# One stock of places for raw weights and their split parts, and a last phase in another order

## The chip, the cores and the metric

The kernel runs on one core of a Trainium2 chip. The core has five engines that run their own instruction streams and wait for one another through semaphores: TensorE (PE in the profile) multiplies matrices, VectorE (DVE) and ScalarE (ACT) work elementwise, GpSimd (POOL) does the same and issues indirect DMAs, SyncE (SP) issues the loads of weights. The metric is the time of one launch on the device in microseconds (us). Three runs of the kernel before took 1482.25, 1484.7 and 1488.44 us; the median is 1484.7.

## The reference

One decoder layer for 512 tokens of width 1024 in float32:

```python
hn = rmsnorm(h, g_mix_norm);  u = hn @ w_in + b_in
ret = silu(rg) * rmsnorm(retention(rq, rk, rv), ret_norm_g)      # 4 heads of 128, chunks of 128
att = sliding_window_attention(aq, ak, av, sinks, bias_table)    # 8 heads of 64, window 128
h = h + concatenate([ret, att]) @ w_out
h = h + moe(rmsnorm(h, g_moe_norm), ...)                         # top 4 of 32 experts
gate = sigmoid(h @ w_ple_gate)
h = h + rmsnorm(gate * (p @ w_ple_proj), g_ple_norm)
return rmsnorm(h, g_final)

def expert(xblk, e):                      # in moe, for the rows routed to expert e
    h = xblk @ w_up[e] + b_up[e]          # 1024 -> 2048
    return clamped_swiglu(h) @ w_down[e] + b_down[e]             # 1024 -> 1024
```

An expert has 8 MB of up weights and 4 MB of down weights, so the 32 experts read 384 MB.

## The kernel before, in words

**Stages.** Input projection, retention and attention take the first 280 us. Then come the output projection w_out, the router and the routing, then the loop over 32 experts, and last the projection of p, the gates and the two closing norms.

**Pieces.** All weights come in pieces of 1 MB (128 partitions x 2048 floats) in one fixed list, `pieces`: per expert eight up pieces and four down pieces, in the list as up(e+1), down(e). `prefetch` takes a raw place from the list `free` and issues the next load on SP's queue; `next_piece` and `whole_piece` take the oldest loaded piece and put its place back behind its last use. There are 3 + 5 + 4 raw places, from the pools rawp, raw2 and raw3.

**Two kinds of experts.** Experts are sorted by their number of tokens when the kernel runs. The table `BIG` says, place by place, which are L (up to 96 rows) and which S (up to 64 rows). An S expert's matmuls read the raw float32 piece directly, in pairs of 64 columns (`pairs64`). For an L expert each piece is split first (`split`): ACT copies it to float32r as wh, DVE subtracts it from the raw piece and writes the remainder wl. PE then makes three products: xTh x wh, xTl x wh and xTh x wl (in a down piece aTh and aTl take the place of xTh and xTl, and a piece holds two blocks of 128 rows, which are done one after the other). The parts wh and wl have pools of their own, whp and wlp with three buffers each, which are used in turn.

**Order.** The program is written out expert by expert: up(e), activation, transposes of the inputs of expert e+1 (`prep` or `prep64`), down(e-1), scatter of its rows into acc, transposes of the activation (`act_t` or `act_t64`). A scheduler orders each engine's instructions from that, with `issue_after` as hints. Each engine runs its own list strictly in that order.

**The end.** At e == E the kernel loads p, splits it, and issues the loads of w_ple_proj and two gate pieces only after the y of expert 30 (`prefetch(after=y)`). It makes three of four projections, reads a flag and branches around a general path for overfull experts, makes the fourth projection, and then runs the gates (i, c) for four token tiles i and two column halves c, with the closing norms (`finish`) between them.

Of the kernel before, what the change touches and what calls it, by code (L numbers as in the profile page):

```python
# [11 lines left out]
F32 = mybir.dt.float32  # L12
# [10 lines left out]
P = 128  # L23
# [13 lines left out]
RAW1, RAW2, RAW3 = 3, 5, 4  # L37
# [9 lines left out]
BIG = [c == "L" for c in "LL" + "SLSLSLSLSLSLSLL" + "SLSLSLSLSLSLLLS"]  # L47
# [48 lines left out]
def hymba_kernel(ctx, tc, x, p, positions, rel_bias_table, g_mix_norm, w_in, b_in, ret_norm_g,  # L96
# [27 lines left out]
    rawp = pool(ctx, "rawp", RAW1)  # L124
    whp = pool(ctx, "whp", 3)
    wlp = pool(ctx, "wlp", 3)
# [7 lines left out]
    R = SimpleNamespace(eid={})  # L134
    free = [rawp] * RAW1

    def raw_tile(dt=F32):
        pl_ = free.pop(0)
        return pl_.tile([P, 2048], dt, name="raw"), pl_

    def split(raw, parts=None, dst=None):
        if dst is None:
            wh = whp.tile([P, 2048], F32R, name="wh")
            wl = wlp.tile([P, 2048], F32R, name="wl")
        else:
            wh, wl = dst
# [51 lines left out]

    pieces = [w_ret(0, 0), w_ret(0, 4), w_kv, w_half(w_in, 0, 2048), w_half(w_in, 4, 2048)]
# [17 lines left out]
    def prefetch(after=None):  # L217
        if free and state["next"] < min(len(pieces), state["limit"]):
            t, pl_ = raw_tile()
# [3 lines left out]
            queue.append((t, pl_))  # L223
            state["next"] += 1

    def next_piece(parts=None, dst=None, more=True):
        t, pl_ = queue.pop(0)
        r = split(t, parts, dst)
        free.append(pl_)
# [3 lines left out]

    def whole_piece(use):

        t, pl_ = queue.pop(0)
        use(t)
        free.append(pl_)
# [88 lines left out]
    raw3 = pool(ctx, "raw3", RAW3)  # L327
    mix = [raw3.tile([P, 2048], F32R, name="raw").rearrange("p (a k t) -> a p k t", a=2, k=KD) for _ in range(NT)]
# [6 lines left out]
    p1 = px.enter_context(ExitStack())  # L335
    actp = pool(p1, "actp")
# [9 lines left out]
    prefetch()  # L346
    nc.sync.dma_start(out=xts[1], in_=x_v[:, 1, :])
    prefetch()
# [116 lines left out]
    def attention(nb):  # L465
# [8 lines left out]
        for gp in range(2):  # L474

            s_ps = [sps.tile([P, 512], F32, name="s_ps").rearrange("p (a b) -> p a b", a=2) for _ in range(2)]
            for g in range(2):
# [800 lines left out]
```

## Time and profile before

| | |
|---|---|
| median of 3 runs | 1484.7 us (1482.25 to 1488.44) |
| profiled execution | 1485.38 us |
| its span, first to last instruction | 1483.6 us |
| mean granted TensorE clock | 0.958 of full speed |
| DMA | 462.47 MB, mean 312 GB/s |

The page gives the busy time of each engine over the span, the costliest groups of instructions and the loads. A query of the trace gives stretches (`windows`: the busy time of each engine in a stretch, the granted clock and the share of the DMA engines) and single instructions (`timeline`: start, duration, and in square brackets how long the engine stood idle before and which instruction released it). A granted clock of 1.00 is 2.4 GHz, 0.50 is 1.2 GHz. Matmuls are pipelined: the time from one start to the next is what one costs, and its duration has the way through the array in it as well.

### The profile page before, as it was taken

What the parts mean: (1) busy time and instruction counts of PE and PEld (TensorE: products, weight loads), DVE (VectorE), ACT (ScalarE), POOL (GpSimd) and SP (SyncE); (2) the same over time, 40 slices, a digit from 0 to 9 for tenths busy, and PEclk for the clock granted to TensorE, in tenths of its full rate; (3) what the DMA queues carried; (4) which work ended last, traced back from release to release, by engine and by line L of the source; (5) the groups of instructions that cost most, each with busy time, mean ns of one, the idle gap of its engine ahead of it and who ended that gap; (6) DMA issues with size and microseconds to landing.
All of it is one profiled execution on the core that took longest, in us unless ns stands there. A gap on an engine that the chain in (4) does not pass through costs nothing. (4 is left out here: it accounts for less than half of the span.)

```text
span 1483.6 us, 16861 instructions
## 1 busy us (share of the span) xinstructions
PE 1351.3 (91%) x6090; PEld 907.1 (61%) x6091; DVE 830.1 (56%) x1005; ACT 677.7 (46%) x750; POOL 224.4 (15%) x238
## 2 busy tenths in 40 slices
PE   5999999588999999999999999999999999999885
PEld 4777777466657474655647657465655647675564
DVE  6637774776547263544637647354553726683356
ACT  5333443455536253543626535343452625573443
POOL 2213241474100000000000000000100000000023
PEclk9999999788999999999999999999999999999998
DMA  9332046667899999999999999999999999987511
GB/s 272 118 109 58 29 142 254 237 254 280 318 402 396 403 405 396 406 399 393 392 396 408 393 388 387 375 403 396 386 394 399 395 387 400 391 328 283 183 72 43
DMA packets 110427, 462.47 MB, mean 312 GB/s; under 512 B 10830, under 2 KB 29180, under 8 KB 77568
## 3 DMA queue, kind: packets, MB, share of 16 engines
q1 hardware_dynamic: 99584, 436.24, 74.8%
q0 software_dynamic: 10320, 24.52, 6.5%
q8 instruction: 49, 0.80, 0.2%
q10 hardware_dynamic: 432, 0.57, 0.1%
q14 instruction: 42, 0.34, 0.1%
HBM read 447.26 MB, written 18.73 MB: 314 GB/s over the span
## 5 line engine op out<-in xcount | busy, mean ns | idle before, releaser
L151 DVE TENSOR_TENSOR wl<-raw,wh 128x2048 fp32r<-128x2048 f32 (+2 forms) x243 | 530.2, 2222 | 151.8 <-ACT wh L150 143.8
L150 ACT ACTIVATE wh<-raw 128x2048 fp32r<-128x2048 f32 (+2 forms) x243 | 442.9, 1858 | 110.2 <-PE up L847 52.2
L864 PE MATMUL up<-raw,xTh 128*64 128x512 f32 x896 | 195.3, 594 | 0.0
L896 DVE TENSOR_SCALAR a<-up 128x512 f32<-128x512 f32 x50 | 32.9, 687 | 267.8 <-ACT sg L895 267.8
L847 PE MATMUL up<-wh,xTh 128*128 128x512 f32 x576 | 162.8, 405 | 9.2 <-ACT wh L150 7.8
L895 ACT ACTIVATE sg<-up 128x512 f32<-128x512 f32 x50 | 27.9, 595 | 297.0 <-issue 158.5
L847 PE MATMUL up<-wl,xTh 128*128 128x512 f32 x576 | 160.9, 401 | 2.2 <-DVE wl L151 2.2
L847 PE MATMUL up<-wh,xTl 128*128 128x512 f32 x576 | 161.0, 401 | 1.4 <-DVE xTl L292 1.4
L864 PEld LDWEIGHTS up<-raw,xTh 128*64 128x64 f32 x896 | 63.1, 137 | 124.6 <-issue 120.0
L847 PEld LDWEIGHTS up<-wh,xTh 128*128 128x128 f32 x576 | 108.7, 191 | 40.5 <-ACT wh L150 13.1
L847 PEld LDWEIGHTS up<-wl,xTh 128*128 128x128 f32 x576 | 109.0, 191 | 32.8 <-DVE wl L151 7.0
L847 PEld LDWEIGHTS up<-wh,xTl 128*128 128x128 f32 x576 | 109.8, 191 | 28.2 <-DVE xTl L292 1.8
L928 PE MATMUL dn<-wh,aTh 128*128 128x512 f32 x288 | 100.8, 434 | 23.8 <-ACT wh L150 23.8
L928 PE MATMUL dn<-wl,aTh 128*128 128x512 f32 x288 | 104.0, 446 | 15.9 <-DVE wl L151 15.9
L942 POOL DMA_INDIRECT acc<-y,slot_i x30 | 45.4, 1514 | 443.3 <-ACT y L937 434.8
L800 POOL DMA_INDIRECT xe<-xg,slot_i x30 | 31.9, 1064 | 485.9 <-PE dn L857 261.0
L864 PE MATMUL dn<-raw,aT 128*64 128x512 f32 x448 | 102.9, 598 | 0.0
L928 PE MATMUL dn<-wh,aTl 128*128 128x512 f32 x288 | 98.2, 425 | 0.0
L928 PEld LDWEIGHTS dn<-wh,aTh 128*128 128x128 f32 x288 | 59.4, 211 | 42.8 <-ACT wh L150 27.3
L928 PEld LDWEIGHTS dn<-wl,aTh 128*128 128x128 f32 x288 | 58.5, 212 | 35.5 <-DVE wl L151 23.1
L914 DVE SCALAR_TENSOR_TENSOR aTl<-tp,aTh 128x512 fp32r<-128x512 f32 x36 | 24.1, 689 | 90.2 <-ACT aTh L913 90.2
L928 PEld LDWEIGHTS dn<-wh,aTl 128*128 128x128 f32 x288 | 59.3, 206 | 15.0
(340 smaller groups left out, 1571.9 us busy)
## 6 DMA issues: line engine op xcount, KB each, us to landing
raw<-in_w_up_dram SPq DMA_DIRECT2D x256, 1024.0 KB, 17.4
raw<-in_w_down_dram SPq DMA_DIRECT2D x128, 1024.0 KB, 17.9
raw<-in_w_in_dram SPq DMA_DIRECT2D x32, 256.0 KB, 4.8
raw<-in_w_out_dram SPq DMA_DIRECT2D x4, 1024.0 KB, 5.0
raw<-in_w_ple_gate_dram SPq DMA_DIRECT2D x4, 1024.0 KB, 10.4
raw<-in_w_in_dram SPq DMA_DIRECT2D x3, 1024.0 KB, 5.7
xt<-in_x_dram SPq DMA_DIRECT2D x4, 512.0 KB, 6.5
h<-in_x_dram POOLq DMA_DIRECT2D x4, 512.0 KB, 7.6
```

The lines of the kernel that those rows point to most:

```text
L150: R.split_act = nc.scalar.activation(to(wh), src(raw), AF.Copy)
L151: R.split_dve = nc.vector.tensor_tensor(out=to(wl), in0=src(raw), in1=to(wh).bitcast(F32), op=ALU.subtract)
L800: return nc.gpsimd.indirect_dma_start(out=dst[0:n, 0:D // h], out_offset=None, in_=xg.rearrange("s (h d) -> (s h) d", h=h), in_offset=bass ...
L847: nc.tensor.matmul(h[n // 2][:, n % 2 * 512:n % 2 * 512 + 512], lhsT=a[:, k, :], rhs=w[:, n * 512:(n + 1) * 512], start=(k == 0 and a is x ...
L864: R.pair = nc.tensor.matmul(o[v * 64:v * 64 + 64, c:c + 512], lhsT=xT[:, k, :], rhs=w[:, v * n + c:v * n + c + 512], start=False, stop=las ...
L895: nc.scalar.activation(sg[:, cs], hv[:, :, 0], AF.Silu, scale=ALPHA)
L896: nc.vector.tensor_scalar(a[:, cs], hv[:, :, 1], LIMIT + 1.0, 1.0 - LIMIT, op0=ALU.min, op1=ALU.max)
L914: nc.vector.scalar_tensor_tensor(flat(l[:, g4, :]), in0=flat(t), scalar=1.0 / ALPHA, in1=flat(h[:, g4, :]).bitcast(F32), op0=ALU.mult, op1 ...
L928: m = nc.tensor.matmul(o[:, n * 512:(n + 1) * 512], lhsT=a[:, k, :], rhs=w[:, kk * 1024 + n * 512:kk * 1024 + (n + 1) * 512], start=False, ...
L942: nc.gpsimd.indirect_dma_start(out=acc.rearrange("s (h d) -> (s h) d", h=h), out_offset=bass.IndirectOffsetOnAxis(ap=idx[0:n, :], axis=0), ...
```

## The change

**One stock.** raw2 has nine places instead of five, and wlp is gone after the first phase. The raw places, the three places of whp and the four of mix (raw3) are 19 places in one stock with two lists, `free` and `spare`. A load takes from `free` first and then from `spare`. A split takes a place each for wh and wl, from `spare` first and then from `free`, and notes the pair in `held`. `used()`, called behind the matmuls of each piece, moves the oldest pair from `held` to `spare`. `room()` decides whether a load may go out: it looks at the next 2 (in the expert loop 3) pieces to be used and keeps two places for each that will be split.

**The front.** The normed rows xn that go to the router take two places of the stock before the loads of w_out are issued. The order of matmuls in attention is tied down with `issue_after`. The slot mask of `route` shares the buffer of sg, and sg and y have one buffer instead of two.

**The loop.** For e == 1 the transposes for expert 2 move from before down(0) to behind it. In `BIG` the last 15 places read SLSLSLLSLLSLLSS instead of SLSLSLSLSLSLLLS, with 18 L and 14 S as before.

**The end.** The loads of w_ple_proj and the gates no longer wait for y. The branch to the general path stands before down(31). All four projections are made in one go, the split of w_ple_proj is cut in four, and the gates follow in the order (0,0) (1,0) (0,1) (1,1) (2,0) (2,1) (3,0) (3,1) with six PSUM buffers instead of four. Some multiplications by g_ple and g_final move from POOL to DVE.

```diff
-RAW1, RAW2, RAW3 = 3, 5, 4
+RAW1, RAW2, RAW3 = 3, 9, 4
-BIG = [c == "L" for c in "LL" + "SLSLSLSLSLSLSLL" + "SLSLSLSLSLSLLLS"]
+BIG = [c == "L" for c in "LL" + "SLSLSLSLSLSLSLL" + "SLSLSLLSLLSLLSS"]
...
-    def raw_tile(dt=F32):
-        pl_ = free.pop(0)
-        return pl_.tile([P, 2048], dt, name="raw"), pl_
+    R = SimpleNamespace(eid={}, wlp=None, depth=2)
+    held = []
+    free = [(rawp, f"a{j}") for j in range(RAW1)]
+    spare = []
+    high = [(whp, f"h{j}") for j in range(3)]
+
+    def raw_tile(dt=F32, name="raw", part=False):
+        first, other = (spare, free) if part else (free, spare)
+        place = (first or other).pop(0)
+        return place[0].tile([P, 2048], dt, name=name, tag=place[1], bufs=1), place
 
     def split(raw, parts=None, dst=None):
-        if dst is None:
-            wh = whp.tile([P, 2048], F32R, name="wh")
-            wl = wlp.tile([P, 2048], F32R, name="wl")
...
+        else:
+            (wh, p0), (wl, p1_) = raw_tile(F32R, "wh", True), raw_tile(F32R, "wl", True)
+            held.append((p0, p1_))
...
+            if not BIG[e]:
+                plain.update(range(len(pieces) - 8, len(pieces)))
         pieces += [w_down_piece(e - 1, f) for f in range(4)]
+        if not BIG[e - 1]:
+            plain.update(range(len(pieces) - 4, len(pieces)))
...
+    def room():
+
+        n = len(free) + len(spare)
+        if R.wlp is not None:
+            return n > 0
+        c = state["next"] - len(queue)
+        ahead = [j not in plain for j in range(c, min(c + R.depth, len(pieces)))]
+        return n > 0 and n + 2 * len(held) > 2 * sum(ahead) - (ahead.index(True) if any(ahead) else 0)
+
+    def prefetch(after=None, n=99):
+        while n and state["next"] < min(len(pieces), state["limit"]) and room():
+            t, place = raw_tile()
...
+    def used():
+        spare.extend(held.pop(0))
+        prefetch()
...
+    xns = [raw_tile(F32, "xn") for _ in range(2)]
     state["limit"] = n_moe
-    while free:
-        prefetch()
-    free.append(b_pool)
+    prefetch()
+    free += [b_pool, high[0]]
     prefetch()
...
                                      rhs=w[:, n * 512:(n + 1) * 512], start=(k == 0 and a is xT[0] and w is wh), stop=False)
+            used()
         R.up_end = add_bias(h, e, 0, 1024, start=False, stop=True)
...
                                              start=False, stop=(k == KD - 1 and w is wl))
+            used()
             if f == 1:
                 R.dn_mid = m
...
-            if e + 1 < E:
+            def turn():
+                return (prep if BIG[e + 1] else prep64)(xe[(e + 1) % 2])
+
+            if e + 1 < E and e != 1:
                 with tc.issue_after(R.up_end.ins):
-                    xT = (prep if BIG[e + 1] else prep64)(xe[(e + 1) % 2])
+                    xT = turn()
...
             state["limit"] = n_moe + 3
-            for _ in range(3):
-                prefetch(after=y)
+            prefetch(n=3)
+            tf, tr = raw_tile(), raw_tile(F32R)
+            general_path(tf[0], tr[0])
...
+        if e == 1:
+            xT = turn()
...
     project(R.dn.tile([P, D], F32, name="dn"), (0,))
     for j in (1, 2):
         project(up_tile(), (j,))
+    project(R.dn.tile([P, D], F32, name="dn"), (3,))
+    used()
     mx.close()
```

ACT's list before, at the passage from an S expert to an L expert in the loop: sg is the activation, xTh and aT are the transposed inputs and activations, y the gated rows, wh the splits.

```order
L895 ACTIVATE sg<-up 128x512
L291 ACTIVATE xTh<-tp 128x512 x2
L150 ACTIVATE wh<-raw 128x2048 x4
L816 ACTIVATE aT_4638<-tp 128x4x2x64
L150 ACTIVATE wh<-raw 128x2048
L937 ACTIVATE y<-dn,slots 128x1024
L150 ACTIVATE wh<-raw 128x2048 x7
```

The same passage in ACT's list after the change:

```order
L158 ACTIVATE wh<-raw 128x2048
L937 ACTIVATE sg<-up 128x512
L319 ACTIVATE xTh<-tp 128x512 x2
L158 ACTIVATE wh<-raw 128x2048 x2
L854 ACTIVATE aT_4252<-tp 128x4x2x64
L158 ACTIVATE wh<-raw 128x2048 x2
L980 ACTIVATE y<-dn,slots 128x1024
L158 ACTIVATE wh<-raw 128x2048 x7
```

The twelve splits are the same, but four that stood together behind xTh are now one ahead of sg, two behind xTh and two behind aT.

SP's list before, from the last loads of w_in (retention) to the first of the experts:

```order
L170 DMA raw<-in_w_in_dram 128x4x128 x24
L156 DMA raw<-in_w_out_dram 128x4x512 x2
L186 DMA raw<-in_w_up_dram 128x2048 x3
L156 DMA raw<-in_w_out_dram 128x4x512 x2
L186 DMA raw<-in_w_up_dram 128x2048 x6
```

And after the change:

```order
L178 DMA raw<-in_w_in_dram 128x4x128 x24
L194 DMA raw<-in_w_up_dram 128x2048
L164 DMA raw<-in_w_out_dram 128x4x512 x4
L194 DMA raw<-in_w_up_dram 128x2048 x9
L809 DMA acc<-h_2019 128x1024
```

The four loads of w_out now stand together, behind one up load, where two of them stood ahead of all up loads.

PE's list before, at the end of up(1): the bias of up(1), the transposes of the input of expert 2 (xe), the bias of down(0) and its first matmuls.

```order
L834 MATMUL up<-bias,sel 128x512 x4
L815 MATMUL tp<-cst,xe_2004 128x128 x4
L834 MATMUL dn<-bias,sel 128x512 x2
L928 MATMUL dn<-wh,aTh 128x512 x2
L928 MATMUL dn<-wh,aTl 128x512 x2
```

The same place after the change:

```order
L872 MATMUL up<-bias,sel 128x512 x4
L872 MATMUL dn<-bias,sel 128x512 x2
L970 MATMUL dn<-wh,aTh 128x512 x2
L970 MATMUL dn<-wh,aTl 128x512 x2
L970 MATMUL dn<-wl,aTh 128x512 x2
```

And the end of down(0) after the change:

```order
L970 MATMUL dn<-wh,aTh 128x512 x2
L970 MATMUL dn<-wh,aTl 128x512 x2
L970 MATMUL dn<-wl,aTh 128x512 x2
L853 MATMUL tp<-cst,xe_2009 128x128 x4
L906 MATMUL up<-raw,xTh 64x512 x32
```

The transposes of xe have moved from ahead of down(0) to behind it, straight before the up matmuls of expert 2.

## Rows read from the trace of the kernel before

**Rows 1.** Page, part 1: busy us (share of the span), instructions.

```profile
PE 1351.3 (91%) x6090; PEld 907.1 (61%) x6091; DVE 830.1 (56%) x1005; ACT 677.7 (46%) x750; POOL 224.4 (15%) x238
```

**Rows 2.** Windows: length, busy of each engine, granted clock, DMA share, GB/s.

```profile
446.00:512.00 66.00, 65.43 (x305) 39.00 (x300) 31.68 (x23) 28.55 (x26) 5.13 (x4) 1.00 1.02 401
...
1300.00:1310.00 10.00, 8.78 (x42) 6.68 (x41) 9.23 (x9) 9.07 (x8) 0.00 (x0) 1.00 0.43 159
```

**Rows 3.** Timeline of SP: start, us, queue, line; first and last of six such rows.

```profile
873.88 12.35 SPq L186 DMA_DIRECT2D raw<-in_w_up_dram  x8
...
1207.24 2.06 SPq L186 DMA_DIRECT2D raw<-in_w_up_dram  x2
```

**Rows 4.** Timeline of ACT in up(1): start, us, [idle before <-releaser].

```profile
351.43 1.92 ACT L150 ACTIVATE wh<-raw 128x2048 fp32r<-128x2048 f32 x1 [0.88 <-PE up L847]
```

**Rows 5.** Timeline of DVE, the wl of the same piece.

```profile
353.38 2.29 DVE L151 TENSOR_TENSOR wl<-raw,wh 128x2048 fp32r<-128x2048 f32 x1 [0.51 <-ACT wh L150]
```

**Rows 6.** Timeline of PE, a down piece whose wl comes late (expert 30).

```profile
1371.52 0.73 PE L928 MATMUL dn<-wl,aTh 128*128 128x512 f32 x2 [1.03 <-DVE wl L151]
1372.09 0.63 PE L928 MATMUL dn<-wh,aTh 128*128 128x512 f32 x2
1372.55 0.63 PE L928 MATMUL dn<-wh,aTl 128*128 128x512 f32 x2
```

**Rows 7.** Timeline of PE, from up(1) over down(0) to up(2).

```profile
361.33 1.09 PE L815 MATMUL tp<-cst,xe 128*128 128x128 f32 x4 [5.55 <-DMA xe<-xg,slot_i]
...
363.07 1.22 PE L928 MATMUL dn<-wh,aTh 128*128 128x512 f32 x2
...
376.83 1.51 PE L864 MATMUL up<-raw,xTh 128*64 128x512 f32 x6
```

**Rows 8.** Timeline of SP, the loads of w_out.

```profile
126.66 45.45 SPq L156 DMA_DIRECT2D raw<-in_w_out_dram  x2
...
217.78 9.97 SPq L156 DMA_DIRECT2D raw<-in_w_out_dram  x2
```

**Rows 9.** Timeline of PE, the first matmul with w_out.

```profile
212.72 0.40 PE L307 MATMUL mm<-wh,raw 128*128 128x512 f32 x1
```

**Rows 10.** Groups of PE by line in the expert loop: matmuls of S experts.

```profile
L864 PE MATMUL up<-raw,xTh 128*64 128x512 f32 x896 | 195.3, 594 | 0.0
...
L864 PE MATMUL dn<-raw,aT 128*64 128x512 f32 x448 | 102.9, 598 | 0.0
```

**Rows 11.** The same view: transposes and biases.

```profile
L911 PE MATMUL tp<-cst,a 128*128 128x128 f32 x128 | 19.9, 283 | 0.0
...
L834 PE MATMUL up<-bias,sel 64*128 64x512 f32 x64 | 11.7, 442 | 0.0
L857 PE MATMUL up<-bias,sel 128*128 128x512 f32 x27 | 9.5, 429 | 0.0
```

**Rows 12.** Timeline of PE, from the last down matmuls into the projection.

```profile
1391.35 1.07 PE L864 MATMUL dn<-raw,aT 128*64 128x512 f32 x2
...
1395.54 0.50 PE L307 MATMUL dn<-wh,raw 128*128 128x512 f32 x1 [2.54 <-ACT wh L150]
...
1406.94 0.50 PE L307 MATMUL dn<-wh,raw 128*128 128x512 f32 x1 [1.16 <-ACTq L1119]
```

**Rows 13.** Timeline of PE, first down piece of an L expert.

```profile
514.62 0.73 PE L928 MATMUL dn<-wh,aTh 128*128 128x512 f32 x2 [2.16 <-ACT wh L150]
...
516.95 1.22 PE L928 MATMUL dn<-wl,aTh 128*128 128x512 f32 x2 [1.00 <-DVE wl L151]
517.97 1.05 PE L928 MATMUL dn<-wh,aTh 128*128 128x512 f32 x2
518.82 1.05 PE L928 MATMUL dn<-wh,aTl 128*128 128x512 f32 x2
```

**Rows 14.** Windows around that down run: the granted clock is third from the end.

```profile
515.50:522.40 6.90, 5.89 (x15) 4.30 (x14) 6.33 (x4) 4.58 (x3) 0.00 (x0) 0.51 1.02 359
522.40:530.00 7.60, 7.60 (x37) 6.16 (x36) 3.59 (x2) 2.40 (x2) 0.00 (x0) 1.00 1.01 417
```

More of the change, by code (lines that the diff above doesn't have):

```diff
@@ L222, in prefetch, with next_piece @@
             pieces[state["next"]](t)
-            queue.append((t, pl_))
+            queue.append((t, place))
             state["next"] += 1
[L226 to L229, printed above, removed]
+            n -= 1
+    def next_piece(parts=None, more=True):
+        t, place = queue.pop(0)
+        r = split(t, parts)
+        free.append(place)
         if more:
@@ L232, in next_piece @@
         return r
+    def used():
+        spare.extend(held.pop(0))
+        prefetch()
     def whole_piece(use):
[L236 removed]
+        t, place = queue.pop(0)
         use(t)
[L238 removed]
+        free.append(place)
         prefetch()
@@ L326, in hymba_kernel @@
     right = ctx.enter_context(ExitStack())
-    raw3 = pool(ctx, "raw3", RAW3)
-    mix = [raw3.tile([P, 2048], F32R, name="raw").rearrange("p (a k t) -> a p k t", a=2, k=KD) for _ in range(NT)]
+    raw3 = pool(ctx, "raw3")
+    mix = [raw3.tile([P, 2048], F32R, name="raw", tag=f"c{j}", bufs=1).rearrange("p (a k t) -> a p k t", a=2, k=KD) for j in range(NT)]
     mm = pool(px, "mm", 2, PSUM)
@@ L476, in attention @@
             s_ps = [sps.tile([P, 512], F32, name="s_ps").rearrange("p (a b) -> p a b", a=2) for _ in range(2)]
+            m = None
             for g in range(2):
                 for kv, rows in enumerate(kvs):
-                    nc.tensor.matmul(s_ps[kv][:, g, 0:nk * P], lhsT=aqT[rows, gp * 2 + g, nb * P:(nb + 1) * P],
-                                     rhs=akT[rows, k0:k0 + nk * P], start=True, stop=True)
+                    with tc.issue_after(m.ins) if m is not None else nullcontext():
+                        m = nc.tensor.matmul(s_ps[kv][:, g, 0:nk * P], lhsT=aqT[rows, gp * 2 + g, nb * P:(nb + 1) * P],
+                                             rhs=akT[rows, k0:k0 + nk * P], start=True, stop=True)
             for kv, rows in enumerate(kvs):
@@ L613, in hymba_kernel @@
     p1.close()
-    raw2 = pool(right, "raw2", RAW2, side="right")
+    R.wlp = None
+    raw2 = pool(right, "raw2", side="right")
     rt = pool(right, "rt", side="right")
-    free += [raw2] * RAW2
+    free += [(raw2, f"b{j}") for j in range(RAW2)]
+    free += high[1:]
     b_raw, b_pool = raw_tile()
@@ L777, in hymba_kernel @@
                 route_tile(i, logits)
+        used()
+        used()
+    free += [t[1] for t in xns]
+    R.depth = 2
+    prefetch()
     def route(posm_ap, v_ap):
-        sm = R.sa.tile([P, NT, P], BF16, name="slot_m")
+        sm = R.sb.tile([P, 512], F32, name="sg", bufs=1).bitcast(BF16)[:, 0:512].rearrange("p (i s) -> p i s", i=NT)
         nc.vector.tensor_tensor(out=sm, in0=iota.rearrange("p (o s) -> p o s", o=1).broadcast_to([P, NT, P]),
@@ L848, in up, with after @@
                                      rhs=w[:, n * 512:(n + 1) * 512], start=(k == 0 and a is xT[0] and w is wh), stop=False)
+            used()
         R.up_end = add_bias(h, e, 0, 1024, start=False, stop=True)
         return h
+    def after(m):
+        return tc.issue_after(m.ins) if m is not None else nullcontext()
     def bias64(o, e, c0):
@@ L876, in down64 @@
         o = R.dn.tile([P, D], F32, name="dn")[:, 0:512]
-        with tc.issue_after(R.up_end.ins), tc.issue_after(R.rows_end.ins):
+        with after(R.up_end), after(R.rows_end):
             bias64(o, e, 1024)
@@ L1097, in hymba_kernel @@
     state["limit"] = len(pieces)
-    w_pr, *ws = [next_piece(more=False) for _ in range(3)]
+    quarters = [(lambda t, k=k: kslice(t, k), lambda t, k=k: kslice(t, k)) for k in range(4)]
+    w_pr = next_piece(quarters, more=False)
+    ws = [[next_piece(more=False) for _ in range(2)]]
     def project(ps, js):
@@ L1180, in hymba_kernel @@
             prefetch()
-    g_ple = bcast(ep2, g_ple_norm[0], D, "g_ple", nc.sync)
-    g_fin = bcast(ep2, g_final, D, "g_fin", nc.sync)
-    ws = [ws]
-    free += [t[1] for t in (last, tmp, tf, tr)]
+    g_ple, g_fin = last[0][:, 0:D], last[0][:, D:2 * D]
+    for dst, src in ((g_ple, g_ple_norm[0]), (g_fin, g_final)):
+        nc.sync.dma_start(out=dst, in_=src.rearrange("(o n) -> o n", o=1).broadcast_to([P, D]))
+    free += [t[1] for t in (tmp,)]
     hT = {}
@@ L1216, in finish @@
         ss = []
+        o = [ep2.tile([P, 512], F32, name="o", bufs=4) for _ in range(2)]
         for c in range(2):
```

199 lines of the change are left out of this document (99 added, 100 removed).

## The prediction

> **What bounds the kernel now.** I read the page first: TensorE (PE) is busy 91% of the span [rows 1]. That alone would make PE the bound, but a share of the span hides the stages, so I read the windows next. In the expert loop PE is busy 65.43 of 66 us and the DMA share is 1.02 at 401 GB/s [rows 2]: both are full, and the question is which one sets the pace. The load queue answers it: eight up pieces of an S expert are issued at 873.88 and again at 1207.24 [rows 3], five S+L pairs later, so a pair takes 333.36 / 5 = 66.7 us and a 1 MB piece 66.7 / 24 = 2.78 us, at a DMA share of 1. Near the end the share drops to 0.43 for 10 us [rows 2], because three L experts in a row do not give places back fast enough. So the loop is paced by the loads, with PE close behind.
>
> Splitting is the third party. In an up run of an L expert ScalarE (ACT) takes 1.92 us per piece for wh and waits only 0.88 us for PE to free a buffer, so it starts every 2.80 us [rows 4]. The subtraction for wl on VectorE (DVE) takes 2.29 us and starts at 353.38, 0.03 us after the wh that began at 351.43 has ended [rows 4, 5]. One piece costs 1.92 + 2.29 = 4.2 us end to end, and the kernel stands 2.8 us per piece only because three buffers let the two engines and PE each work on another piece.
>
> **What the change does to that.** Parts wh and wl now come from one stock; `split` asks `raw_tile(part=True)`, which takes from `spare` as long as `spare` holds anything, and only then from `free`. Who fills `spare`? Only `used()`, which puts back the two places of a piece behind that piece's matmuls, and in program order this is before the next piece is split. So the next split finds exactly the pair just given back and takes it again. More than one pair can be in `spare` only if several splits were made without `used()` between them, as the three at the start of the loop are; then three pairs rotate through experts 0 and 1. But the first S expert's loads, which take `free` and then `spare`, empty `spare`, and raw places return to `free`. At the next L piece `spare` is empty, one pair is taken from `free`, and from then on all 12 pieces of every run (four down, eight up) use one pair, although `room()` holds back loads to leave six places for parts: these lie in `free`, which a part does not look at first. The kernel before rotates three in both pools.
>
> With one pair the write of wh of a piece waits for the wl of the piece before (DVE reads that wh) and for PE's last matmul on that wh. The order shows the same thing from its side: between the last S piece and the L run four wh could stand together, now one, then two and two.
>
> Cycle of an up piece: wh 1.92, hop 0.03, wl 2.29, hop about 0.05: 4.29 us. PE's eight wh matmuls (8 x 0.234 = 1.9 us) fit inside the 2.29; a matmul is 0.234 us since two start 0.46 us apart [rows 6].
>
> Cycle of a down piece: its matmuls go wh, wh, wl for the first half of the rows and again for the second, so wh is read until the tenth of twelve. After wl is there, six matmuls must run: from 1371.52 to 1372.55 + 0.63 = 1373.18, 1.66 us [rows 6]. So 1.92 + 0.03 + 2.29 + 0.06 + 1.66 + 0.06 = 6.02 us. Both were 2.8.
>
> **The sum.** Against the profiled execution of 1485.38 us (span 1483.6 and 1.8 around it; the median of the runs is 1484.7).
> - Expert 2 starts its up run at 376.83 [rows 7]. Three things move it. The transposes for expert 2, which stood ahead of down(0) and waited 5.55 us for the gather, move behind it: from 361.33 to the first down matmul at 363.07 the 1.7 us of transposes go as well, but come back later in part: -5 together [rows 7]. The fourth piece of down(0) has to wait for the third: 6.02 - 2.8 = +3.2. The w_out loads: two were issued at 126.66, while now all four wait for places that retention's last matmuls on act_l free (they end just before 212.72 [rows 8, 9]; the sync engine's queue holds one up load ahead of them); a load and a split lie between that and the first w_out matmul, which ran at 212.72. PE has the rest of retention, moved ahead of it, to do meanwhile, which hides most; I take +6 from bounds of 0 (all hidden) and 14 (the 212.72 shifted to about 227, behind the second pair of loads at 217.78 plus land and split). Start: 376.8 - 5 + 3.2 + 6 = 381.
> - L up, experts 3 and on: 16 x 8 x 4.29 = 549. L down from expert 1 on: 17 x 4 x 6.02 = 409.
> - S experts use raw pieces, unchanged: 195.3 up and 102.9 down [rows 10].
> - Transposes and bias matmuls outside the L down runs: 19.9 + 11.7 + 9.5 = 41 [rows 11]; the others fall into PE's new gaps.
> - Joints: the pair for the first down piece is free once the seventh S piece is done, so the eighth (195.3 / 112 = 1.74) covers it; at the end of an up run four wl matmuls (0.93) remain. 16 x (-1.74 + 0.93) = -13.
>
> 381 + 549 + 409 + 195 + 103 + 41 - 13 = 1665 for the end of the last down, before 1392.
> - The last phase took 1483.6 - 1392.4 = 91.2. Loads no longer wait for the last y, so the 2.54 us before the projection goes [rows 12], and so does the 1.16 us at the branch in the middle of it. Gates behind all projections and six buffers may give some 5 more: -9 between -3 and -15. That is 82.
> - 1665 + 82 + 1.8 = 1749 at the full clock.
>
> The loads do not bind then: 66.7 us per pair against 8 x 4.29 + 4 x 6.02 + 21.3 (S) = 80. The larger stock only gives the loads more to lie in, and the new order of the last experts is worth nothing while DMA waits.
>
> **The clock.** Before, each pair has one first piece of a down run that arrives late: PE waits 2.16 us for wh at 514.62 and 1.00 us for wl at 516.95, and then two pairs of matmuls stand 0.85 us apart [rows 13], a granted clock of 0.51 (1.2 of 2.4 GHz) for 6.9 us, back to 1.00 once the pieces are ready [rows 14]. After the change all four pieces of a down run come like that, so I take the fall to hold through the run. A matmul is then 0.427, the six behind wl cost 6 x 0.193 = 1.16 more, three pieces of four 3.5, and one or two of the next up pieces (eight wh matmuls 3.42 against 2.32 for DVE) 1.1 each: 5 per L expert, 17 x 5 = 85. Sum: 1834.
>
> The Trainium skill, page "TensorE: Matmul & The Clock Gate", section "A second HAM failure mode: psum-queue depth-cycling", says that short but frequent pauses between groups of matmuls suffice to send the clock up and down; its section "HAM oscillation — how this bites in real kernels" ties the fall to one long wait per tile. By the first the 85 belongs in the sum, by the second it does not (1749). Rows 13 and 14, where two short waits preceded the fall, side with the first.
>
> **Rivals.**
> 1. The clock holds at 1.00 in the down runs: 1749. For it: PE still works half of each cycle; against: the 0.51 after two such waits.
> 2. The clock stays low in the up runs too: every up piece +1.1, 16 x 7 x 1.1 = 123 more, 1950. Against: at half clock PE would have 12 x 0.427 = 5.1 us of work in 5.4, and the clock came back in such a stretch [rows 14].
> 3. Faster: several pairs do rotate in `spare`, because splits run ahead of `used()` or places wander otherwise than I follow. It decides from two pairs on: the split cycle falls below 3.78 us per L piece ((66.7 - 21.3) / 12; one pair gives (8 x 4.29 + 4 x 6.02) / 12 = 4.87), and the loads bind again. Then the six to seven places more let loads run some 6 x 2.78 = 16 us further ahead, the new order saves the hole near the end (10 x 0.57 = 6), the last phase 9: about 1455. Against: `used()` stands in the program ahead of every next split.
> 4. The stock helps nobody and nothing serializes: within a few us of 1485. For it only that the loads bind anyway.
>
> **Chances.** Forecast 0.62, first rival 0.15, second 0.12, third 0.07, fourth 0.04. Less than 0.5% (7 us) cannot be told from no change here. Faster 0.07, same 0.02 and slower 0.91 (half of the fourth rival falls to each of the last two). The forecast's own range is 1800 to 1870; taking in the first rival and most of the second, 1735 to 1945.
>
> **What would show it.** In a run of an L expert ACT's wh must start 4.3 us apart in up and 6 to 7.2 in down, each behind a DVE wl (up) or PE dn (down); a pair of experts takes 80 us or more; the DMA share in the loop sinks to about 0.8; down rows of PE show 0.85 us per two matmuls; the last down ends near 1750. wh 2.8 us apart and a DMA share of 1 would refute the whole account. The first w_out matmul near 220 to 227 checks the front, no 2.54 us ahead of the projection checks the end.

## The result and the profile after

The changed kernel takes 1754.35 us (median of 4 runs, 1749.36 to 1757.16), the kernel before 1485.3 us on the same chip. The ratio is 1.1808, with a 95% interval of 1.1768 to 1.1847. The sign was forecast. The time lies inside the wide range (1735 to 1945) and outside the forecast's own (1800 to 1870): 80 us below the likeliest number (1834) and 5 above the first rival (1749, the clock holds). The profiled execution took 1749.36 us, with a span of 1747.6.

Part 1 of the page of the changed kernel answers to [rows 1]:

```profile
PE 1443.4 (83%) x6090; PEld 881.5 (50%) x6091; DVE 839.6 (48%) x1013; ACT 690.3 (39%) x754; POOL 243.6 (14%) x227
```

The instructions are the same but for a few, and PE's share falls from 91 to 83%. DVE and ACT are busy only 10 and 13 us longer. PE, with the same number of matmuls, is counted busy 92 us longer (why is not worked out here) and idle 172 us longer: the engines wait. The list of waits of the changed kernel says for whom (waiting engine and line, releaser, us in all, times, longest; L158 is now the copy to wh, L159 the subtraction to wl, L970 the L experts' down matmuls):

```profile
DVE wl L159 <- ACT wh L158: 612.7, 210, 17.1
...
ACT wh L158 <- PE dn L970: 250.4, 60, 5.3
ACT wh L158 <- DVE wl L159: 243.3, 101, 2.5
```

The third row is new in kind: before, wh waited for PE to free one of three buffers [rows 4]; now it waits for the wl of the piece before, 101 times 2.4 us, and DVE waits for wh in turn (143.8 us before, 612.7 now). ACT's timeline of the changed kernel, in an up run and in the down run behind it (start, us, what, idle before and releaser), shows the cycle:

```profile
606.58 1.91 ACT L158 ACTIVATE wh<-raw 128x2048 fp32r<-128x2048 f32 x1 [2.41 <-DVE wl L159]
610.90 1.91 ACT L158 ACTIVATE wh<-raw 128x2048 fp32r<-128x2048 f32 x1 [2.41 <-DVE wl L159]
...
661.88 1.91 ACT L158 ACTIVATE wh<-raw 128x2048 fp32r<-128x2048 f32 x1 [2.61 <-PE dn L970]
667.87 1.91 ACT L158 ACTIVATE wh<-raw 128x2048 fp32r<-128x2048 f32 x1 [4.08 <-PE dn L970]
673.86 1.91 ACT L158 ACTIVATE wh<-raw 128x2048 fp32r<-128x2048 f32 x1 [3.60 <-PE dn L970]
681.11 1.91 ACT L158 ACTIVATE wh<-raw 128x2048 fp32r<-128x2048 f32 x1 [5.34 <-PE dn L970]
```

Up pieces stand 4.32 us apart (forecast 4.29) and down pieces 5.99 (forecast 6.02), each behind the releaser that was named. The last gap is 7.25. DVE's row in that up run answers to [rows 5]; its wait was 0.51 us there:

```profile
608.53 2.29 DVE L159 TENSOR_TENSOR wl<-raw,wh 128x2048 fp32r<-128x2048 f32 x1 [2.03 <-ACT wh L158]
```

PE in the same down run answers to [rows 13]:

```profile
663.84 0.74 PE L970 MATMUL dn<-wh,aTh 128*128 128x512 f32 x2 [1.53 <-ACT wh L158]
...
666.17 0.73 PE L970 MATMUL dn<-wl,aTh 128*128 128x512 f32 x2 [1.12 <-DVE wl L159]
...
678.15 1.22 PE L970 MATMUL dn<-wl,aTh 128*128 128x512 f32 x2 [1.12 <-DVE wl L159]
679.17 1.05 PE L970 MATMUL dn<-wh,aTh 128*128 128x512 f32 x2
680.02 1.05 PE L970 MATMUL dn<-wh,aTl 128*128 128x512 f32 x2
```

The second to the fourth piece come late, with two waits each, yet pairs of matmuls stand 0.85 us apart only in the fourth. Windows of the changed kernel show it by clock (length; busy PE, PEld, DVE, ACT, POOL; granted clock, DMA share, GB/s), the first two being whole pairs of experts, the third most of the up run above, the last two the second and third piece and then the fourth piece of that down run:

```profile
599.90:683.10 83.20, 67.05 (x274) 36.52 (x274) 33.98 (x23) 29.97 (x26) 7.15 (x4) 0.98 0.85 317
683.10:767.10 84.00, 68.50 (x273) 37.30 (x273) 33.92 (x22) 29.90 (x26) 7.16 (x4) 0.96 0.84 313
606.58:633.67 27.09, 21.15 (x78) 13.32 (x78) 13.75 (x6) 11.48 (x6) 0.00 (x0) 1.00 0.74 248
664.00:676.00 12.00, 7.12 (x29) 4.71 (x30) 4.60 (x3) 4.31 (x3) 0.00 (x0) 1.00 1.02 390
676.00:681.00 5.00, 3.88 (x11) 2.77 (x12) 2.10 (x1) 0.00 (x0) 0.00 (x0) 0.67 0.67 249
```

These pairs take 83 to 84 us and load 313 to 317 GB/s (before, 66.7 us from [rows 3] and 401 GB/s in [rows 2]): the loads no longer set the pace.

The front is later than forecast. SP of the changed kernel, answering to [rows 8], and PE's first matmul with w_out, answering to [rows 9]:

```profile
215.28 0.34 SPq L194 DMA_DIRECT2D raw<-in_w_up_dram  x1
215.72 3.97 SPq L164 DMA_DIRECT2D raw<-in_w_out_dram  x4
...
275.92 0.33 SPq L808 DMA_DIRECT2D xg<-xn  x1
```

```profile
233.56 0.79 PE L335 MATMUL mm<-wh,raw 128*128 128x512 f32 x1 [2.80 <-ACT wh L158]
```

All four loads of w_out are issued behind 215, and its first matmul runs 20.8 us later than before. (By these rows w_out begins well inside the first 280 us, which the description of the stages gives to the input projection, retention and attention alone.) The first store of xn goes out at 275.92 (258.27 before) and the first up run starts at 316.1 (299.1 before): 17 us of the 20.8 come through.

At the end, PE of the changed kernel answers to [rows 12]:

```profile
1670.99 0.50 PE L335 MATMUL up<-wh,raw 128*128 128x512 f32 x1
```

The projection follows the last down matmul with no wait, the 2.54 and 1.16 us are gone, and the phase from there to the end takes 76.5 us instead of 91.2. The first gate, at 1685.60, waits 2.30 us for its transposed input (0.73 before).

### The profile page after: what moved, and what is told of

Same layout as the page of the kernel before. It is cut to its first block, busy times and chain, and to the rows that moved or that the text cites. A ratio compares the mean times of both kernels' runs of the same rounds, so it can differ in the third digit from the quotient of the medians.

```text
span 1747.6 us, 16919 instructions
## 1 busy us (share of the span) xinstructions
PE 1443.4 (83%) x6090; PEld 881.5 (50%) x6091; DVE 839.6 (48%) x1013; ACT 690.3 (39%) x754; POOL 243.6 (14%) x227
## 5 line engine op out<-in xcount | busy, mean ns | idle before, releaser
L159 DVE TENSOR_TENSOR wl<-raw,wh 128x2048 fp32r<-128x2048 f32 (+2 forms) x247 | 543.1, 2201 | 650.5 <-ACT wh L158 612.7
L158 ACT ACTIVATE wh<-raw 128x2048 fp32r<-128x2048 f32 (+2 forms) x247 | 452.7, 1836 | 682.8 <-PE dn L970 250.4
L885 PE MATMUL up<-wh,xTh 128*128 128x512 f32 x576 | 174.4, 424 | 107.3 <-ACT wh L158 105.6
L906 PE MATMUL up<-raw,xTh 128*64 128x512 f32 x896 | 208.1, 601 | 0.7 <-ACT xTh L854 0.7
L885 PE MATMUL up<-wl,xTh 128*128 128x512 f32 x576 | 172.0, 420 | 23.8 <-DVE wl L159 23.8
L885 PEld LDWEIGHTS up<-wh,xTh 128*128 128x128 f32 x576 | 99.5, 191 | 178.6 <-ACT wh L158 161.6
L970 PE MATMUL dn<-wl,aTh 128*128 128x512 f32 x288 | 111.5, 472 | 43.4 <-DVE wl L159 43.0
L885 PEld LDWEIGHTS up<-wl,xTh 128*128 128x128 f32 x576 | 99.4, 190 | 92.7 <-DVE wl L159 78.0
L970 PE MATMUL dn<-wh,aTh 128*128 128x512 f32 x288 | 106.3, 453 | 47.3 <-ACT wh L158 47.3
L838 POOL DMA_INDIRECT xe<-xg,slot_i x30 | 50.7, 1689 | 618.3 <-PE dn L899 351.5
L985 POOL DMA_INDIRECT acc<-y,slot_i x30 | 60.9, 2029 | 530.5 <-ACT y L980 530.5
L970 PEld LDWEIGHTS dn<-wl,aTh 128*128 128x128 f32 x288 | 56.6, 217 | 88.2 <-DVE wl L159 67.2
L970 PE MATMUL dn<-wh,aTl 128*128 128x512 f32 x288 | 98.9, 427 | 0.0
L970 PEld LDWEIGHTS dn<-wh,aTh 128*128 128x128 f32 x288 | 53.7, 206 | 86.6 <-ACT wh L158 69.7
L970 PEld LDWEIGHTS dn<-wh,aTl 128*128 128x128 f32 x288 | 59.8, 208 | 15.0
L906 PEld LDWEIGHTS dn<-raw,aT 128*64 128x64 f32 x448 | 31.2, 138 | 59.5 <-issue 58.9
```

Of the source, the lines that this page charges most:

```text
L158: R.split_act = nc.scalar.activation(to(wh), src(raw), AF.Copy)
L159: R.split_dve = nc.vector.tensor_tensor(out=to(wl), in0=src(raw), in1=to(wh).bitcast(F32), op=ALU.subtract)
L838: return nc.gpsimd.indirect_dma_start(out=dst[0:n, 0:D // h], out_offset=None, in_=xg.rearrange("s (h d) -> (s h) d", h=h), in_offset=bass ...
L885: nc.tensor.matmul(h[n // 2][:, n % 2 * 512:n % 2 * 512 + 512], lhsT=a[:, k, :], rhs=w[:, n * 512:(n + 1) * 512], start=(k == 0 and a is x ...
L906: R.pair = nc.tensor.matmul(o[v * 64:v * 64 + 64, c:c + 512], lhsT=xT[:, k, :], rhs=w[:, v * n + c:v * n + c + 512], start=False, stop=las ...
L970: m = nc.tensor.matmul(o[:, n * 512:(n + 1) * 512], lhsT=a[:, k, :], rhs=w[:, kk * 1024 + n * 512:kk * 1024 + (n + 1) * 512], start=False, ...
```

## The experiments

**Theory A**: with one pair of places in turn for wh and wl, ACT, DVE and PE work one after the other, and this is the whole loss. **Rival B**: the loss has other sources too (the larger stock, the new order, the clock), and giving the pairs back brings only a part. A ratio is to the kernel before on the same chip.

### Three pairs set aside (e1_three_pairs)

From the fourth split on, the first one inside the expert loop, splits take their places from a list of their own, into which `used()` returns them. Three pairs rotate in it, and 13 places are left for loads, which `room()` no longer holds back.

```diff
-        place = (first or other).pop(0)
+        place = (R.pairs if part and R.kept else first or other).pop(0)
...
-        if R.wlp is not None:
+        if R.wlp is not None or R.kept:
...
-        spare.extend(held.pop(0))
+        (R.pairs if R.kept else spare).extend(held.pop(0))
...
+    R.kept = True
```

> The changed kernel, but from the third split of the loop on three pairs of places are set aside for wh and wl and used in turn, so the loads have the other 13 of the 19 places. Theory (one pair in turn with itself serializes ACT, DVE and PE, and this alone costs the time): an L run goes back to about 2.8 us per piece, the loads bind again at 66 to 67 us per pair of experts, and the front (about +15) and the last phase (about -15) of the changed kernel stay: 1455 to 1490 us. Rival (holding back loads, the order of L and S or the front cost a good part): over 1550 us, with L runs that wait for loads.

Measured: 1492.56 us, ratio 1.0059 [1.004, 1.0077]. ACT's timeline and a window of this kernel:

```profile
621.32 1.93 ACT L158 ACTIVATE wh<-raw 128x2048 fp32r<-128x2048 f32 x1 [0.89 <-PE up L885]
624.13 1.93 ACT L158 ACTIVATE wh<-raw 128x2048 fp32r<-128x2048 f32 x1 [0.88 <-PE up L885]
```

```profile
446.00:512.00 66.00, 66.00 (x307) 39.60 (x305) 34.92 (x25) 31.78 (x29) 5.85 (x5) 1.00 1.02 402
```

Back are the 2.81 us per piece, the 0.88 us of waiting for PE, and the loads as the pace; the time is 2.6 us above the range that was expected. Of the change only the single pair and the holding back of loads in `room()` are out, so some 262 us hang on these two, nearly all of the loss, and B falls but for `room()`. The next run leaves `room()` as it is. What is left is +9 us in the medians and +2.9 in the profiled executions. I put it down to the late front (first up run at 315.6, 16.5 us late) less the shorter last phase (82.6 us, 8.6 less).

### One list for all (e2_one_list)

`used()` returns the pair to `free`, where loads and parts both take.

```diff
-        spare.extend(held.pop(0))
+        free.extend(held.pop(0))
```

> The changed kernel, but the pair of a piece goes back to the list that loads take from, at its end, and parts take from its front, so nothing else than the place that a part gets is different. Theory: wh of a piece then goes to a place that was last read one or two pieces earlier; most up pieces come 2.8 to 3 us apart, first pieces of down runs still about 4.3 apart; pairs of experts 67 to 71 us, 1460 to 1540 us in all. Rival (the time is lost elsewhere): 1740 us or more.

Measured: 1524.93 us, ratio 1.0267 [1.0242, 1.0291]. A single word decides 229 us, with everything else of the change still in, `room()` too: what serialized was that a split looks first at the list into which the last pair has just gone. So A holds for at least these 229 of the 269 us. The 32 us that remain above e1 are not settled by this run; the loads that `room()` holds back here, and not in e1, may have a part in them. In its trace some wh still start behind DVE's wl, 4.27 us after the one before (598.52 and 602.79); I read this as a part that took the oldest free place and got one not yet done.

### The order of the down matmuls (e3_down_order)

On the changed kernel; wh is then read for the last time by the eighth of twelve matmuls, not the tenth.

```diff
-            for kk in range(2):
-                k = f * 2 + kk
-                for a, w in ((aT[0], wh), (aT[1], wh), (aT[0], wl)):
+            for a, w in ((aT[0], wh), (aT[1], wh), (aT[0], wl)):
+                for kk in range(2):
+                    k = f * 2 + kk
```

> The changed kernel, but within a down piece the matmuls go wh x aTh for both blocks of rows, then wh x aTl for both, then wl x aTh for both, so that wh is read for the last time by the eighth matmul instead of the tenth, and ahead of the matmuls on wl. Theory: the down cycle falls from 6.0 us to 4.3 us (wh and wl only), at four places per L run, 17 runs: 1754 - 4 x 17 x 1.67 = 1640 us (1630 to 1665). Rival (down runs are bound by the transposes between them or the clock): within 15 us of 1754.

Measured: 1650.2 us, ratio 1.1115 [1.1088, 1.1142], 104 us less than the changed kernel. ACT in a down run of this kernel, and its core view (span, mean granted clock):

```profile
644.73 1.91 ACT L158 ACTIVATE wh<-raw 128x2048 fp32r<-128x2048 f32 x1 [1.93 <-PE dn L970]
649.05 1.91 ACT L158 ACTIVATE wh<-raw 128x2048 fp32r<-128x2048 f32 x1 [2.41 <-DVE wl L159]
```

```profile
core 0: 1646.7 us, clock 0.979
```

Down pieces go from 5.99 to 4.32 us, the cycle of an up piece. So the extra 1.66 us of the down cycle was PE's six matmuls behind wl, as worked out. They are not all of the 104 us. The mean granted clock is 0.979, where the changed kernel has 0.959 (shown below): 2 x 0.021 x 1646.7 = 69 us at half clock instead of 143, so up to half of the difference, 37 us, can be the clock's.

### One pair in the kernel before (e4_before_one_pair, e5_before_one_pair_again)

The converse: take the kernel before and let one pair rotate from expert 2 on.

```diff
+            turns = 3 if R.one else 1
...
-            wh = whp.tile([P, 2048], F32R, name="wh")
+            wh = [whp.tile([P, 2048], F32R, name="wh") for _ in range(turns)][0]
...
+        R.one = 2 <= e < E
```

> The kernel before, but from the loop's third expert on each split writes the same one buffer for wh and the same one for wl, instead of three in turn; nothing else differs. Theory: the cost is in the single pair, whatever the stock and the order: L up cycle 4.3 us, L down cycle 6.0 us, pairs of experts 83 us instead of 66.7, so 1485 + 15 x 16.7 = 1735 us (1715 to 1760). Rival (it takes the new lists or the new order as well): below 1600 us, since ACT and DVE are busy for about half the time.

Measured: 1485.94 us, ratio 1.0007 [0.9987, 1.0027]. This says nothing on the theory: the surplus tiles were never written and took no buffer, and in the trace the up pieces stand 2.80 us apart as before (612.67 and 615.47). The second attempt names the buffers and fixes the turn, with the same condition for `R.one`:

```diff
+            R.turn = 0 if R.one else (R.turn + 1) % 3
-            wh = whp.tile([P, 2048], F32R, name="wh")
+            wh = whp.tile([P, 2048], F32R, name="wh", tag=f"h{R.turn}", bufs=1)
...
```

> The run before this one on the same question kept three buffers in turn (the surplus tiles of its edit took no buffer), so it said nothing. Here each buffer of the kernel before has a name of its own, and from the loop's third expert on every split writes the same pair. Theory: the single pair alone costs the time, in the kernel before as well: L up cycle 4.3 us, L down cycle 6.0 us, a pair of experts about 83 us instead of 66.7; 1485 + 15 x 16.7 = 1735 us (1715 to 1760). Rival (it takes the new lists, the held loads or the new order too): below 1600 us.

Measured: 1768.66 us, ratio 1.1902 [1.187, 1.1935]. ACT's timeline of this kernel, in an up and a down run and at the first piece of another down run:

```profile
603.40 1.91 ACT L151 ACTIVATE wh<-raw 128x2048 fp32r<-128x2048 f32 x1 [2.41 <-DVE wl L152]
607.72 1.91 ACT L151 ACTIVATE wh<-raw 128x2048 fp32r<-128x2048 f32 x1 [2.41 <-DVE wl L152]
...
655.74 1.91 ACT L151 ACTIVATE wh<-raw 128x2048 fp32r<-128x2048 f32 x1 [4.09 <-PE dn L930]
662.99 1.91 ACT L151 ACTIVATE wh<-raw 128x2048 fp32r<-128x2048 f32 x1 [4.86 <-PE dn L930]
```

```profile
631.85 1.91 ACT L151 ACTIVATE wh<-raw 128x2048 fp32r<-128x2048 f32 x1 [7.46 <-DMA raw<-in_w_down_dram]
```

With nothing else of the change in it, the kernel before shows the same 4.32 us, and down gaps of 6.00 to 7.25: the loss needs no other part of the change. The time is 34 us above the likeliest number and 9 above the range. Late loads do not explain this. ACT waits for the load of a first down piece ten times, 72 us in all, as in the last row; but PE is then in the up run of an S expert (until 645.71 in that case) and starts the down run right behind it, at 647.10. What was too small is the count: it had 15 pairs at 16.7 us, 250 in all. From the first S up run to the last down matmul PE's rows give 284 us more than before: 221 over the 13 L experts in the middle (17.0 each), 12 for the down run of expert 1, and 51 for the last three L experts, which stand in a row.

### The front (e6 to e9)

With the pairs back, the late front is what costs. e6 is e1 with the first two loads of w_out issued early again:

```diff
-    xns = [raw_tile(F32, "xn") for _ in range(2)]
     state["limit"] = n_moe
+    prefetch(n=2)
+    xns = [raw_tile(F32, "xn") for _ in range(2)]
```

> Three pairs of places in turn as in the first run, and the two places for xn are taken from the stock after the first two loads of w_out are issued instead of before, so that these go to places that are free early. Theory: the first up run, which started about 17 us later than in the kernel before, starts within 3 us of 299 us again; since the loads bind afterwards most of that reaches the end: 1492.6 - 12 = 1480 us (1472 to 1485). Rival (the front was late for another reason, the order of retention's matmuls): within 4 us of 1492.

Measured: 1486.45 us, ratio 1.0006 [0.9992, 1.002]; expected was 1480, at most 1485. The first w_out matmul is back at 211.27 and the first store of xn at 261.02, but the first up run starts at 313.8. POOL's timeline of this kernel says why:

```profile
302.63 1.12 POOL L1039 DMA_INDIRECT slot_d<-pay,dest  x1 [9.59 <-DVE dest L1036]
...
307.92 1.00 POOL L839 DMA_INDIRECT xe<-xg,idx  x1 [0.30 <-issue]
```

The gather of expert 0's rows now stands behind four scatters of the routing; in the kernel before it was issued at 288.75, ahead of them all. Also the fourth xn is stored at 293.05 (283.62 before), and two tiles serve all four stores. So the 15 us that the early loads give back at the first store are lost again further on.

e7 is e6 with the `BIG` of before, e8 is e6 with two pairs set aside instead of three (15 places for loads):

```diff
-        (R.pairs if R.kept else spare).extend(held.pop(0))
+        (R.pairs if R.kept and len(R.pairs) + 2 * len(held) <= 4 else free).extend(held.pop(0))
```

> As the run with three pairs and early w_out loads, but the last 15 experts in the order of the kernel before (three L in a row near the end). Theory: the order only matters where the loads have a hole; three L in a row leave one of about 6 us near 1300 us: 4 to 8 us more than with the new order. Rival (the place of the L experts has no influence since the loads bind over all): within 2 us.

> As the run with three pairs and early w_out loads, but only two pairs of places are in turn, and the loads have 15 places instead of 13. Theory: two pairs are enough: with two, a split waits for the piece two before, half of 4.3 or 6.0 us per piece, under PE's 2.8 and the loads' 2.78 (down runs 3.0 at most); loads bind, and two more places for them change little: within 8 us of the run with three pairs. Rival (the third pair hides ACT's other work in the run: activations, transposes): 15 to 40 us more.

Measured: e7 1490.82 us (1.0028 [1.0015, 1.0042]), e8 1486.57 us (1.0003 [0.9989, 1.0017]). The new order of the last experts is worth 4.4 us. Giving up the third pair for two more places for loads changes nothing here; what each would do alone is not told apart.

e9 is e6 with both causes of the late front removed: four xn tiles (two places in halves), and the scatters tied behind the gathers.

```diff
-                xn = xns[i % 2][0][:, 0:D]
+                xn = xns[i // 2][0][:, i % 2 * D:(i % 2 + 1) * D]
...
-            nc.gpsimd.indirect_dma_start(
...
+            with tc.issue_after(R.last_pool.ins):
+                nc.gpsimd.indirect_dma_start(
+                    out=slot_d[k], out_offset=bass.IndirectOffsetOnAxis(ap=dest[:, i * 4 + k:i * 4 + k + 1], axis=0),
...
```

> The run with three pairs and early w_out loads, and in addition the gathers of experts 0 and 1 are issued on POOL's queue ahead of the scatters of the slot tables instead of behind four of them, and the four xn tiles share two places by halves, so none waits for another. In the run before this one PE stood 15.4 us for that gather, whose index was ready at 291.4 and which POOL issued at 307.9. Theory: that order, not the w_out loads, made the rest of the late front: the first up run starts near 300 us (before the change 299) instead of 313.8, and 1486.5 - 11 = 1475 us (1468 to 1481). Rival (the front is hidden anyway, since the loads bind afterwards): the first up run starts early, but the time stays within 3 us of 1486.

Measured: 1472.34 us, ratio 0.9906 [0.9891, 0.9921]. POOL's timeline of this kernel:

```profile
289.81 1.11 POOL L839 DMA_INDIRECT xe<-xg,idx  x1 [0.94 <-DVE ig L832]
```

The first scatter follows at 299.15, and the first up run starts at 298.5. Of the 15 us gained there 14 reach the end. The two edits were made together; what each gives is not told apart.

### Down order and two pairs on the mended kernel (e10 to e12)

e10 is e9 with the down order of e3 and the two pairs of e8; e11 is e9 with the down order alone, e12 with the two pairs alone. The diffs are those above.

> As the run with the gather first, with two pairs in turn (15 places for loads) and with the down matmuls in the order that gives wh back after eight of twelve. Theory: both only matter where splits bind, and they do not any more: within 4 us of the run with the gather first. Rival (the start of the down runs, where the first pieces come late and the clock falls, is worth something): 5 to 15 us less than that run.

> One of the two edits of the run that reached 1444.9: the gather-first kernel with three pairs (13 places for loads) and the down matmuls in the new order. The first piece of each down run comes late and costs PE one wait for wh and one for wl; in the new order PE has four matmuls instead of two to do on wh while wl is made, so a place comes back earlier and loads follow earlier. Theory A (the order of the matmuls is the gain): 1442 to 1452 us. Theory B (the two places more for loads are the gain): within 5 us of 1472. If the two add up: about 1458.

> The other edit alone: the gather-first kernel with two pairs in turn, so 15 places for loads, and the down matmuls in the order of both original kernels. Theory A (the order of the matmuls is the gain): within 5 us of 1472. Theory B (the loads could not run far enough ahead near the end, where the DMA share was 0.95 to 0.97 after 1150 us with 13 places and 1.00 with 15): 1442 to 1452 us. If the two add up: about 1458.

Measured: e10 1444.94 us (0.9726 [0.9708, 0.9745]), e11 1451.93 (0.9782 [0.9761, 0.9803]), e12 1471.72 (0.9899 [0.9877, 0.992]). e10 came out 27 us below e9, more than either theory had: both had priced the down order too low. e11 and e12 take it apart: the order alone gives 20, two pairs instead of three (15 places for loads instead of 13) alone nothing, and the same on top of the order 7. PE at the start of a down run, first in e9:

```profile
639.46 0.73 PE L971 MATMUL dn<-wh,aTh 128*128 128x512 f32 x2 [2.10 <-ACT wh L158]
640.03 0.63 PE L971 MATMUL dn<-wh,aTl 128*128 128x512 f32 x2
641.79 1.22 PE L971 MATMUL dn<-wl,aTh 128*128 128x512 f32 x2 [1.13 <-DVE wl L159]
642.81 1.05 PE L971 MATMUL dn<-wh,aTh 128*128 128x512 f32 x2
```

and the same in e11:

```profile
634.73 1.20 PE L971 MATMUL dn<-wh,aTh 128*128 128x512 f32 x4 [2.10 <-ACT wh L158]
635.76 1.09 PE L971 MATMUL dn<-wh,aTl 128*128 128x512 f32 x4
637.05 1.20 PE L971 MATMUL dn<-wl,aTh 128*128 128x512 f32 x4 [0.20 <-DVE wl L159]
```

With eight wh matmuls to do while DVE makes wl, the second wait shrinks from 1.13 to 0.20 us, and in this run the clock does not fall behind it (in another down run of this kernel, from 570.05 on, it does). The rows of the waits (us in all, times, longest), first of e9:

```profile
PE dn L971 <- DVE wl L159: 12.4, 11, 1.1
```

and of e11:

```profile
PE dn L971 <- DVE wl L159: 1.2, 6, 0.2
```

The core view (span, mean granted clock) of e9:

```profile
core 0: 1470.7 us, clock 0.962
```

of e10:

```profile
core 0: 1444.5 us, clock 0.970
```

and of e11:

```profile
core 0: 1449.7 us, clock 0.975
```

Time at half clock is twice what the mean lacks of 1, times the span: 112 us in e9 (2 x 0.038 x 1470.7), 87 in e10, 72 in e11. The 40 us less in e11 are up to 20 us of PE's time, and the shorter waits are another 11 us. Together that is more than the 20 us which the order gives, so part of it does not reach the end, and how the 20 divide between wait and clock is not told apart. That the second wait is the trigger for the clock is not shown either: in e10, PE's row at 638.91 has four such matmuls in 1.91 us, half clock, behind the 2.10 us wait alone.

```profile
637.59 1.51 PE L971 MATMUL dn<-wh,aTh 128*128 128x512 f32 x4 [2.10 <-ACT wh L158]
638.91 1.91 PE L971 MATMUL dn<-wh,aTl 128*128 128x512 f32 x4
```

e10 beats both kernels: 2.7% faster than the one before.

## Why the prediction was right, and where it failed

**Right: the mechanism.** One pair in turn, wh behind wl, PE behind both; a cycle of 4.29 and 6.02 us, measured 4.32 and 5.99; pairs above 80 us; a DMA share of 0.85 where about 0.8 was named. e2 and e5 show it from both sides, e1 with the loads set free as well. The rival of several pairs in turn and the one of no effect fall with the rows at 606.58 to 673.86. The one of a low clock in the up runs falls with the window from 606.58, whose granted clock is 1.00 (its sum is 1834 + 123 = 1957 and not 1950). Three of the signs that were named did not come: the last down matmul ends at 1671 and not near 1750, pairs of down matmuls 0.85 us apart are the exception, and the first w_out matmul runs at 233.6 and not between 220 and 227.

**Failed: the clock term.** "After the change all four pieces of a down run come like that, so I take the fall to hold through the run ... 5 per L expert, 17 x 5 = 85." The row at 663.84 and those behind it show that it does not hold: three of the four pieces come late, and in that run only one of these is at half clock, which makes its gap 7.25 instead of 5.99 us. A clock of 0.98 and 0.96 in the two pairs is 3.3 and 6.7 us at half clock (2 x 0.02 x 83.2, 2 x 0.04 x 84.0), so at most half of that, 1.7 to 3.4 us, is lost in each. Two later pairs are worse; one of them:

```profile
1068.48:1153.72 85.24, 70.22 (x273) 38.51 (x273) 33.96 (x23) 29.93 (x26) 7.17 (x4) 0.94 0.86 327
```

That is 10.2 us at half clock, and the pair takes 2.0 us more than the one of 83.20. The eight plain pairs (S and L in turn, the down run alone) take 84.0 us on average (671.7 us for eight, from PE's timeline), where the terms give 81.5 without the clock. So the clock can have cost at most 2.5 us per pair on average and not 5, some 30 us for the twelve L experts whose down run stands alone; in the other five it did not fall at all (1.00 in each of their windows). The term was 85. Nor is half clock new: the kernel before, with a mean of 0.958, has 2 x 0.042 x 1483.6 = 125 us at half clock, and the changed one 2 x 0.041 x 1747.6 = 143 by its core view:

```profile
core 0: 1747.6 us, clock 0.959
```

The step took the one clock fall of [rows 13, 14] for the rule of every late piece.

The prediction sided with one of two sections of the Trainium skill, page "TensorE: Matmul & The Clock Gate": "A second HAM failure mode: psum-queue depth-cycling" (short, frequent pauses suffice), against "HAM oscillation — how this bites in real kernels" (one long wait per tile). This trace agrees with neither alone: two pauses of 1.1 to 1.5 us per piece left the clock at 1.00 in the second and third piece (against the first section), and it fell in the fourth though no wait was longer than in the second (against the other). In e3, with waits of 0.2 to 1.1 us in a down run, the clock stays at 1.00 over whole pairs. What decides stays open.

**Missed: down pieces between S pieces.** I summed every L down run as one that stands alone. Where two L stand in a row, the scheduler now puts the first one's down pieces between the up pieces of the next S expert (at the very end, where two S follow, the second one's too). PE of the changed kernel:

```profile
1018.71 0.73 PE L970 MATMUL dn<-wh,aTh 128*128 128x512 f32 x2
1019.29 0.63 PE L970 MATMUL dn<-wh,aTl 128*128 128x512 f32 x2
1019.84 1.94 PE L906 MATMUL up<-raw,xTh 128*64 128x512 f32 x8
1021.71 0.72 PE L970 MATMUL dn<-wl,aTh 128*128 128x512 f32 x2
```

The S matmuls fill the wait for wl: from 1012.85 to 1042.89 an S up run (14.0 us alone) and the down run are both done in 30.0 us, so the down run costs 16 instead of 24. There are five such, some -40 us.

**The other terms.** The front was put at +6 with bounds of 0 and 14 on the loads of w_out: the direction was right, but the first matmul moved by 20.8 us, not 14, and the rest of retention hid little of it, so the up run of expert 2 starts at 390.6, not 381. An L up run takes 33.8 us (34.3 forecast). The last phase was put at 82 us and took 76.5, near the end of the bound of -15.

Counted from the forecast: 1834, less the clock term of 85, plus 30 for what the plain pairs really took, less 40 for the five runs between S pieces, plus 10 at the start, less 5.5 at the end, plus 6.5 that I cannot put to single places, gives 1750; the profiled execution took 1749.36. That the first rival's 1749 lies beside it is luck: what it left out cancels (loop 1280.5 against its 1284, start +10, last phase -5.5), and its condition, a clock of 1.00 in the down runs, did not hold either.

## What to carry to other kernels

A stock that prefers the place just given back turns several buffers into one: ask which place the next allocation gets in program order, and not how many there are. With the stages of a piece worked out from single rows (1.92 + 2.29, and six matmuls), the price of that is good to 1%. What follows from the clock is not (85 forecast, at most some 30 found), so such a term belongs in the range; and before runs are summed as standing alone, look at the order of the engine for what lies between them.

## What the runs showed that I had not expected

- The order of twelve matmuls within a down piece is worth 104 us with one pair (e3, where the granted clock also rises from 0.959 to 0.979) and 20 us with three (e11, where it rises from 0.962 to 0.975). Two pairs instead of three, with two more places for loads, are worth 7 us with the new order and nothing with the old (e10, e12).
- The granted clock fell behind waits of 1.5 and 1.1 us in one piece and not in the two before it, whose waits were 1.5 and 1.1 us and 1.1 and 1.1.
- A gather behind four scatters on POOL, and two tiles where four stores are made, together kept a front 15 us late whose first store was back within 3 us of the old time (e6, e9).
